# First layer of the NSA compression in a decoder trunk: one matmul of 512 columns for the high and low weights together, in place of two of 256

## The chip, the cores and the metric

The kernel runs on one core of one Trainium2 chip. The metric is device time in microseconds (us) for one execution: before the change the median of three runs is 1060.82 us (1060.35 to 1060.99). The profiled execution, from which all durations here are read, took 1061.77 us, with a span of 1060.0 us between its first and its last instruction.

The engines are named as in the profile: PE is the matmul engine (PEld its weight loads), DVE the vector engine, ACT the scalar engine, POOL and SP the two that mostly start transfers. The profile's "x" behind a row counts instructions, and a pair such as 128x512 gives partitions and elements of each.

## The reference, cut to what matters

One layer of a decoder trunk for 256 positions and 2048 channels in fp32: a normalised input goes through one wide projection `w_in`; three branches (a linear recurrence, A; sparse attention in the NSA manner, B; attention with a forget gate, C) each give 1024 channels; each branch is multiplied by its own gate, projected by `w_branch`, weighted by a merge gate, and the sum goes through `w_out`. The change lies in branch B, in the compressed blocks:

```python
def compress(t, pos, w1, w2):
    ...
    blocks = jnp.concatenate([chunks[:, r:r + n_cmp] for r in range(ratio)], axis=2)
    blocks = blocks + pos[:, None, :]
    flat = blocks.transpose(0, 1, 3, 2, 4).reshape(b, n_cmp, hk, CMP_BLOCK * dk)
    return jax.nn.silu(flat @ w1) @ w2
...
    k_c = rms_norm(compress(split_heads(z['nsa_k_cmp'], NSA_KV_HEADS), cmp_pos[l, 0],
                            cmp_w1[l, 0], cmp_w2[l, 0]), nsa_k_gain[l])
    v_c = compress(split_heads(z['nsa_v_cmp'], NSA_KV_HEADS), cmp_pos[l, 1],
                   cmp_w1[l, 1], cmp_w2[l, 1])
```

There are 15 blocks for each of 2 heads; `w1` is 4096 x 256, once for keys and once for values. Branch A's output, which matters for what follows, is `rglru_branch(...) * silu(z['lru_gate'])`, and it is the first that is projected.

## The kernel before, in words

**Numbers in two parts.** A fp32 product is made of the short format's matmuls: each operand is split into a high part (ACT rounds a copy) and a low part (DVE subtracts it from the original), and high·high, high·low and low·high are summed in PSUM (`mm3`, line 384).

**Pieces.** All weights come as one stream of pieces of at most 128x1024 (`plan`, line 76). A piece is loaded into `raw`, split into `wh` (ACT) and `wl` (DVE) by `cut` (line 418), and used by a few matmuls. Splitting runs three pieces ahead of use (`AHEAD`), in four buffers each for `wh` and `wl`. ACT's part is issued at the start of a piece; DVE's subtraction of the same later piece is put off to the middle of the current piece (`low_parts`, line 413). A piece of 512 columns by 2 rows of blocks has 12 matmuls.

**The first layer of the compression** (lines 1350 to 1361) is spread between the pieces of `w_in`: 8 pieces for keys, then 8 for values, each with 4 blocks of 128 rows by 256 columns. Its input `k_xs` has 60 columns, 30 high and 30 low ones, so that one matmul against `wh` and one against `wl` give all products; both accumulate in one half of a PSUM bank, keys in columns 0 to 255, values in 256 to 511. When the values are done, `cmp_end` (line 829) copies the bank to `hs`, transposes it, adds the 30 low rows to the 30 high ones, and goes on to the second layer.

**Side work and its order.** Everything that isn't a weight piece (recurrence, norms, attention, splitting of the branch outputs) is written as tasks that are advanced in small steps. Instructions stand in each engine's queue in the order in which this program writes them, so the order is fixed when the kernel is built. A clock in the kernel (`Clock`, line 158) adds up a cost for each instruction on each engine. After the first half and at the end of every piece, `Side.tick` (line 257) gives each urgent and each active task one step, unless that clock holds DVE or ACT to be further behind PE than a limit (`LIMITS`: 3000 ns for urgent tasks, 2500 ns for the others, from the first attention queries on). Tasks also wait by that clock until what they need would be done.

**What a piece needs.** Before a piece is written, `need` (line 1281) looks whether the tasks whose results it reads have been written, and if not, it steps all tasks regardless of the limit until they are:

```python
        for name in wait:
            n = 0
            while name not in side.done:
                n += 1
                assert n < 2000, name
                clock.t["pe"] += 200.0
                side.tick(True)
```

**The first projection.** `ysplit0` (`y_split`, line 1102) makes branch A's output: in four quarters of 128x512, DVE multiplies `k_yl` by the gate `k_gl`, ACT rounds it to `k_yh`, and DVE subtracts to `k_yl` (another buffer of that name). A quarter may be written once the four `lru` tasks are done. The first column block of `w_branch` has four pieces, and piece number i needs quarter number i. Ahead of that block stands the first block of merge gates, whose result DVE and ACT turn into `k_mg` (line 1213).

Of the kernel before, what the change touches and what calls it, by code (L numbers as in the profile page):

```python
# [11 lines left out]
R32 = mybir.dt.float32r  # L12
AF = mybir.ActivationFunctionType
OP = mybir.AluOpType
AX = mybir.AxisListType

P = 128
# [9 lines left out]
NCMP = 15  # L27
NR = 32
HID = 256
# [296 lines left out]
def block_kernel(ctx: ExitStack, tc: tile.TileContext, io):  # L326
    nc = tc.nc
    clock = Clock()
    V, A, T, G, Q = (Metered(e, clock, n) for e, n in ((nc.vector, "v"), (nc.scalar, "a"), (nc.tensor, "pe"),
                                                      (nc.gpsimd, "g"), (nc.sync, "d")))  # L330
    pool = lambda name, bufs=1, **k: ctx.enter_context(tc.tile_pool(name=name, bufs=bufs, **k))
    cp = pool("cp")
    wp = pool("wp")
# [11 lines left out]
    def nm(s):  # L345
        uid[0] += 1
        return f"{s}_{uid[0]}"
# [7 lines left out]
    def two(shape, dt=F32, name="b2"):  # L355
        return k2.tile(shape, dt, tag="k2", name=nm("k2_" + name))
# [7 lines left out]
    def f(ap):  # L364
        return ap.bitcast(F32)

    mains = [pp.tile([P, 512], F32, name=f"main{i}") for i in range(4)]
    banks = [pp.tile([P, 512], F32, name=f"bank{i}") for i in range(4)]
# [12 lines left out]
    def split(hi, lo, src, scale=None):  # L381
        splits((hi, lo, src, scale))
# [11 lines left out]
    def parts_of(h, k, nk):  # L394

        n = h["n"]
        if h is halves[0] and k == 0:
            return [(0, n // 2), (n // 2, n)]
        return [(k * n, (k + nk) * n)]
# [13 lines left out]
    def low_parts():  # L413

        while due:
            V.tensor_tensor(*due.pop(0), op=OP.subtract)

    def cut(h, k=0, nk=None, late=False):
        m, n = h["nk"] * h["n"], h["n"]
        nk = nk or h["nk"]  # L420
        if k == 0:
            h["whl"] = [wp.tile([P, 1024], R32, tag=x, bufs=AHEAD + 1, name=nm(x)) for x in ("wh", "wl")]
        wh, wl = h["whl"]
        for a, b in parts_of(h, k, nk):
            if late:
                A.activation(wh[:, a:b], h["raw"][:, a:b], AF.Copy)
                due.append((wl[:, a:b], h["raw"][:, a:b], f(wh[:, a:b])))
            else:
                split(wh[:, a:b], wl[:, a:b], h["raw"][:, a:b])
        h["wh"] = wh[:, :m].rearrange("p (k n) -> p k n", n=h["n"])  # L430
        h["wl"] = wl[:, :m].rearrange("p (k n) -> p k n", n=h["n"])
# [44 lines left out]
    def halves_of(pairs_):  # L476
        return lambda k: (pairs_[k // 8][0][:, k % 8, :], pairs_[k // 8][1][:, k % 8, :])


    st = {}  # L480
# [29 lines left out]
    for i in range(4):  # L510
        for k in range(2):
            if i < FINE or k == 0:
                n = 1 if i < FINE else 2
# [315 lines left out]
    def cmp_end():  # L829
        b = st["cmpb"]  # L830
        w2 = two([P, 2, 2, P], name="w2")
        G.dma_start(w2, io["w2"])
        hs = two([4 * NCMP, 512], name="hs")
        A.activation(hs, banks[b][:4 * NCMP, :], AF.Copy)
        yield from side.settle()

        for q in range(4):
# [3 lines left out]
        hz = banks[b][:, :4 * 4 * NCMP].rearrange("p (q s i) -> p q s i", q=4, s=2)  # L841
# [14 lines left out]
        for q in range(2):  # L856
            T.matmul(banks[b][:64, 256:256 + P], hid2[:, q].rearrange("p g c i -> p (g c i)"), w2[:, 1, q, :],
                     start=q == 0, stop=q == 1)
# [438 lines left out]
    def prepare(j):  # L1297

        for ks in ([0], [1]) if j < FINE else (range(2),):
            if "pair" in halves[j]:  # L1300
                hn_first(halves[j]["pair"], ks)
            if j < FINE:
                cut(halves[j], ks[0], 1)
        if j >= FINE:
            cut(halves[j], late="q0" in side.done)
# [4 lines left out]
    for i, h in enumerate(halves):  # L1310
# [28 lines left out]
        if kind == "ple":  # L1339
            out = by_rows(h, lambda k: (pTh[:, k, :], pTl[:, k, :]))  # L1340
        elif kind in ("rows", "turned"):
            out = by_rows(h, halves_of(hn))
        elif kind == "proj":
            out = by_rows(h, lambda k: (st["ys"][0][:, k, :], st["ys"][1][:, k, :]))
        elif kind == "out":
            out = by_rows(h, halves_of(st["mt"]))
        elif kind == "gate":
            out = by_rows(h, halves_of(st["ht"]))
        else:
            kv = h["key"]  # L1350
            if h["first"] and kv == 0:
                st["cmpb"] = side.free.pop(0)[0]
            for k in range(h["nk"]):
                if 2 * k == h["nk"]:
                    low_parts()
                for q, w in enumerate((h["wh"], h["wl"])):
                    T.matmul(banks[st["cmpb"]][:4 * NCMP, kv * HID:(kv + 1) * HID], st["xs"][kv][:, h["k"] + k, :],
                             w[:, k, :], start=h["first"] and k == 0 and q == 0 and kv == 0,
                             stop=h["last"] and k == h["nk"] - 1 and q == 1 and kv == 1)
            if h["last"] and kv == 1:  # L1360
                side.urge("cmpend", cmp_end())
        if h["last"]:
# [28 lines left out]
RAW, LOADS, AHEAD = 6, 7, 3  # L1391
# [88 lines left out]
```

## Time and profile before

| | before |
|---|---|
| median of three runs | 1060.82 us |
| the profiled execution | 1061.77 us |
| its span | 1060.0 us |
| PE busy | 1053.3 us (99%) |
| DVE busy | 772.2 us (73%) |
| ACT busy | 620.6 us (59%) |
| granted clock | 0.999 |

Matmuls overlap in their pipeline: a row of 512 columns lasts 0.39 us, but the next one starts 0.227 us later. So PE's share of busy time says little, and the distance from one start to the next is what has to be read. The chain of waits (the work that ended last, followed backwards) names runs of matmuls by where they write: "main" for the four banks of the weight pieces, "bank" for the four that side work and the first layer of the compression use. A line of the program is of no use as a key, since one helper records every instruction (L208); groups are told apart by the names of the tiles.

### The profile page before, as it was taken

To read this page: it belongs to the slowest core of one execution; us is meant where nothing else is said; L and a number is where in the kernel's file an instruction comes from. 1 tells how busy PE (TensorE), PEld (TensorE's weight loads), DVE (VectorE), ACT (ScalarE), POOL (GpSimd) and SP (SyncE) were. 2 spreads that over 40 slices of the span, in tenths; PEclk is the share of its full clock that TensorE was granted. 3 is DMA by queue.
4 is the path that set the end of the run, shared out by engine and by line. 5 is a ranking of instruction groups with operands and counts; after the bars stand their busy time and mean duration, and the time that the engine had idled before them with its cause. 6 is when DMAs were issued, how large, how long until landed. Compare 5 with 4: busy or idle time off the path is not lost.

```text
span 1060.0 us, 14061 instructions
## 1 busy us (share of the span) xinstructions
PE 1053.3 (99%) x4903; PEld 879.3 (83%) x4903; DVE 772.2 (73%) x1151; ACT 620.6 (59%) x940; POOL 53.1 (5%) x77
## 2 busy tenths in 40 slices
PE   9999999999999999999999999999999999999998
PEld 7888889888888888888888888888888888888886
DVE  7777889897778678678987965555766566766664
ACT  7668877768766667544645644555555444444442
POOL 0000001110000000020110000000001000000000
PEclk9999999999999999999999999999999999999999
DMA  9767868787657467577677566766676877778751
GB/s 337 248 201 260 257 200 280 233 266 226 217 189 218 150 198 216 182 234 251 194 235 239 186 222 207 223 213 214 219 244 196 264 235 220 236 250 257 278 207 60
DMA packets 86295, 237.52 MB, mean 224 GB/s; under 512 B 14024, under 2 KB 31312, under 8 KB 86224
## 3 DMA queue, kind: packets, MB, share of 16 engines
q1 hardware_dynamic: 81504, 220.87, 64.8%
q0 software_dynamic: 4720, 15.76, 5.5%
q8 instruction: 38, 0.62, 0.3%
q14 instruction: 33, 0.27, 0.1%
HBM read 215.61 MB, written 4.20 MB: 207 GB/s over the span
## 4 chain that ended last, share of the span: by engine, by line
PE 91%; DVE 3%; DMA 2%; ACT 2%; SPq 1%; issue 1%; DVEq 0%; ACTq 0%
PE main L208 87%; PE bank L208 4%; SPq L208 1%; DVE wl L208 1%; DMA raw<-in_w 1%; DMA k_fpz<-k_fprob 1%; DMA k_pz<-k_prob 1%; ACT wh L208 0%; ACT k_pz L208 0%; DVE k_fq L208 0%; DVE k_prob L208 0%; DVE k_fprob L208 0%; DVE k_pt L208 0%; DVE k_fbias L208 0%; DVE k_fx L208 0%
## 5 line engine op out<-in xcount | busy, mean ns | idle before, releaser
L208 DVE TENSOR_TENSOR wl<-raw,wh 128x1024 fp32r<-128x1024 f32 (+2 forms) x388 | 459.8, 1197 | 186.0 <-ACT wh L208 185.2
L208 ACT ACTIVATE wh<-raw 128x1024 fp32r<-128x1024 f32 (+2 forms) x388 | 400.2, 1040 | 318.3 <-PE main L208 281.3
L208 PE MATMUL main<-wh,k_hnh 128*128 128x512 f32 (+2 forms) x1026 | 395.0, 385 | 0.5 <-ACT wh L208 0.5
L208 PE MATMUL main<-wh,k_hnl 128*128 128x512 f32 (+1 forms) x1024 | 393.0, 384 | 0.0
L208 PE MATMUL main<-wl,k_hnh 128*128 128x512 f32 (+2 forms) x1026 | 392.9, 384 | 0.0
L208 PEld LDWEIGHTS main<-wh,k_hnh 128*128 128x128 f32 x1026 | 193.2, 189 | 37.5 <-ACT wh L208 1.1
L208 PEld LDWEIGHTS main<-wh,k_hnl 128*128 128x128 f32 x1024 | 192.5, 188 | 38.1
L208 PEld LDWEIGHTS main<-wl,k_hnh 128*128 128x128 f32 x1026 | 193.2, 189 | 35.9 <-DVE wl L208 0.2
L208 PE MATMUL main<-wl,k_yh 128*128 128x512 f32 x192 | 74.9, 390 | 0.1
L208 PE MATMUL main<-wh,k_yh 128*128 128x512 f32 x192 | 74.9, 390 | 0.0
L208 PE MATMUL main<-wh,k_yl 128*128 128x512 f32 x192 | 74.8, 389 | 0.0
L208 PE MATMUL main<-wh,k_mth 128*128 128x512 f32 x128 | 49.8, 389 | 0.0
L208 PE MATMUL main<-wl,k_mth 128*128 128x512 f32 x128 | 49.8, 389 | 0.0
L208 PE MATMUL main<-wh,k_mtl 128*128 128x512 f32 x128 | 49.8, 389 | 0.0
L208 PE MATMUL main<-wh,k_hth 128*128 128x512 f32 x128 | 49.8, 389 | 0.0
L208 PE MATMUL main<-wl,k_hth 128*128 128x512 f32 x128 | 49.8, 389 | 0.0
L208 PE MATMUL main<-wh,k_htl 128*128 128x512 f32 x128 | 49.8, 389 | 0.0
L208 PEld LDWEIGHTS main<-wl,k_yh 128*128 128x128 f32 x192 | 36.0, 188 | 7.7 <-DVE wl L208 0.5
L208 PEld LDWEIGHTS main<-wh,k_yl 128*128 128x128 f32 x192 | 36.0, 188 | 7.5
L208 PEld LDWEIGHTS main<-wh,k_yh 128*128 128x128 f32 x192 | 36.1, 188 | 7.4
L208 ACT ACTIVATE k_mg<-k_mg 128x512 f32<-128x512 f32 x24 | 15.2, 633 | 26.6 <-DVE k_mg L208 26.3
L208 PEld LDWEIGHTS main<-wl,k_mth 128*128 128x128 f32 x128 | 24.0, 188 | 5.0
(243 smaller groups left out, 948.4 us busy)
## 6 DMA issues: line engine op xcount, KB each, us to landing
raw<-in_w SPq DMA_DIRECT2D x369, 512.0 KB, 4.5
bias<-in_b_in POOLq DMA_DIRECT2D x21, 256.0 KB, 5.2
raw<-in_w SPq DMA_DIRECT2D x8, 408.0 KB, 4.0
k_pz<-k_prob SPq DMA_DIRECT2D x16, 128.0 KB, 4.2
e_dram<-k_e POOLq DMA_DIRECT2D x4, 512.0 KB, 3.6
k_merged<-k_zt SPq DMA_DIRECT2D x16, 128.0 KB, 3.2
k_xc<-in_x POOLq DMA_DIRECT2D x4, 512.0 KB, 6.4
k_hx<-k_zt SPq DMA_DIRECT2D x16, 128.0 KB, 3.6
```

The source lines that it names most:

```text
L208: r = call(out, *args, **kw)
```

## The change

`wh` and `wl` become the two halves of one tile `whl`. The first layer's two matmuls for a block of 128 rows become one with 512 moving columns, the 256 high and the 256 low weights, and its 512 results fill the whole bank: high products in the left half, low ones in the right. So keys and values can't share the bank any more. After the last piece of the keys, and again after that of the values, ACT copies the left half to `hs` and DVE adds the right half; `hs` is now taken before the first piece, and its copy in `cmp_end` is gone.

```diff
@@ cut
-            h["whl"] = [wp.tile([P, 1024], R32, tag=x, bufs=AHEAD + 1, name=nm(x)) for x in ("wh", "wl")]
-        wh, wl = h["whl"]
+            h["whl"] = wp.tile([P, 2, 1024], R32, tag="whl", bufs=AHEAD + 1, name=nm("whl"))
+        wh, wl = h["whl"][:, 0], h["whl"][:, 1]
@@ cmp_end
-        hs = two([4 * NCMP, 512], name="hs")
-        A.activation(hs, banks[b][:4 * NCMP, :], AF.Copy)
+        hs = st["hs"]
@@ the pieces of the first layer
                 st["cmpb"] = side.free.pop(0)[0]
+                st["hs"] = two([4 * NCMP, 512], name="hs")
+            hz = banks[st["cmpb"]][:4 * NCMP, :].rearrange("p (s n) -> p s n", s=2)
             for k in range(h["nk"]):
                 if 2 * k == h["nk"]:
                     low_parts()
-                for q, w in enumerate((h["wh"], h["wl"])):
-                    T.matmul(banks[st["cmpb"]][:4 * NCMP, kv * HID:(kv + 1) * HID], st["xs"][kv][:, h["k"] + k, :],
-                             w[:, k, :], start=h["first"] and k == 0 and q == 0 and kv == 0,
-                             stop=h["last"] and k == h["nk"] - 1 and q == 1 and kv == 1)
+                T.matmul(hz, st["xs"][kv][:, h["k"] + k, :], h["whl"][:, :, k * HID:(k + 1) * HID],
+                         start=h["first"] and k == 0, stop=h["last"] and k == h["nk"] - 1)
+            if h["last"]:
+                part = st["hs"][:, kv * HID:(kv + 1) * HID]
+                A.activation(part, hz[:, 0], AF.Copy)
+                V.tensor_tensor(part, part, hz[:, 1], op=OP.add)
```

Because the kernel's own clock counts the shorter first layer and the two additions, the steps of the side work fall at other places from the first layer on, until some 640 us into the span. Three places show what the prediction speaks of.

First, PE's queue at the first piece of the first layer, before the change. `k_xs` is the input in its 60 columns, and the rows read "output <- weights, input":

```order
L208 MATMUL main_84<-wh_721,k_hnl_129 128x512
L208 MATMUL bank_90<-wh_743,k_xs_644 60x256
L208 MATMUL bank_90<-wl_744,k_xs_644 60x256
L208 MATMUL bank_90<-wh_743,k_xs_644 60x256
L208 MATMUL bank_90<-wl_744,k_xs_644 60x256
L208 MATMUL bank_90<-wh_743,k_xs_644 60x256
L208 MATMUL bank_90<-wl_744,k_xs_644 60x256
L208 MATMUL bank_90<-wh_743,k_xs_644 60x256
L208 MATMUL bank_90<-wl_744,k_xs_644 60x256
L208 MATMUL main_83<-wh_765,k_hnh_128 128x512
```

And the same place after it:

```order
L208 MATMUL main_84<-whl_696,k_hnh_128 128x512 x2
L208 MATMUL main_84<-whl_696,k_hnl_129 128x512
L208 MATMUL bank_90<-whl_717,k_xs_622 60x512 x4
L208 MATMUL main_83<-whl_738,k_hnh_128 128x512 x2
L208 MATMUL main_83<-whl_738,k_hnl_129 128x512
```

Eight matmuls of 256 columns have become four of 512; nothing else moved here.

Second, DVE's queue around the first projection, before the change. `k_yl<-k_yl,k_gl` is the multiplication of a quarter, `k_yl<-k_yl,k_yh` its low part, `wl<-raw,wh` the low part of a weight piece, `k_mg` the merge gates. The first pair is that of the fourth quarter; the other three stand further up:

```order
L208 TENSOR_TENSOR k_yl_567<-k_yl_567,k_gl_980 128x512
L208 TENSOR_TENSOR k_yl_2769<-k_yl_567,k_yh_2768 128x512
L208 TENSOR_TENSOR wl_2912<-raw_2818,wh_2911 128x1024
L208 SCALAR_TENSOR_TENSOR k_mg_2930<-main_85,rsr,bias_2796 128x512
L208 SCALAR_TENSOR_TENSOR k_mg_2931<-main_86,rsr,bias_2796 128x512
L208 TENSOR_TENSOR wl_2939<-raw_2839,wh_2938 128x1024
L208 TENSOR_TENSOR wl_2957<-raw_2857,wh_2956 128x1024
L208 TENSOR_TENSOR wl_2975<-raw_2883,wh_2974 128x1024
```

After it. The first two quarters stand ahead of these rows, and the pairs shown are those of the third and the fourth; `sp_sm`, `k_pc` and `k_pz` belong to a step of an attention task:

```order
L208 SCALAR_TENSOR_TENSOR k_mg_2787<-main_86,rsr,bias_2650 128x512
L208 TENSOR_TENSOR whl_2794<-raw_2702,whl_2794 128x1024
L208 TENSOR_TENSOR whl_2811<-raw_2727,whl_2811 128x1024
L208 TENSOR_TENSOR k_yl_548<-k_yl_548,k_gl_936 128x512
L208 TENSOR_TENSOR k_yl_2755<-k_yl_548,k_yh_2754 128x512
L208 TENSOR_SCALAR sp_sm_2564<-sp_sm_2564 128x6
L208 RECIPROCAL sp_sm_2564<-sp_sm_2564 128x6
L208 TENSOR_TENSOR sp_sm_2564<-sp_sm_2564,bg 128x6
L208 SCALAR_TENSOR_TENSOR k_pc_361_2566<-sp_pc_2565,sp_sm_2564,k_pc_361_2566 128x2x16
L208 TENSOR_SCALAR k_pz_2568<-k_pz_2568,sp_sm_2564 128x4x32 x2
```

The last two rows come once more, and then the two of the fourth quarter. Two of the four quarters have moved from ahead of the merge gates to behind them and behind two low parts of weight pieces, and a step of attention stands between the two.

Third, PE's queue where the third piece of the first projection begins, after the change (`kk` are keys, `k_qh` and `k_ql` queries):

```order
L208 MATMUL main_84<-whl_2746,k_yl_2755 128x512
L208 MATMUL bank_87<-kk,k_qh_2490 128x272 x2
L208 MATMUL bank_87<-kk,k_ql_2491 128x272
L208 MATMUL bank_89<-kk,k_qh_2490 128x256 x2
L208 MATMUL bank_89<-kk,k_ql_2491 128x256
L208 MATMUL main_83<-whl_2768,k_yh_2754 128x512 x2
L208 MATMUL main_83<-whl_2768,k_yl_2755 128x512
```

Before the change that piece follows the second one directly:

```order
L208 MATMUL main_84<-wh_2885,k_yh_2768 128x512
L208 MATMUL main_84<-wl_2886,k_yh_2768 128x512
L208 MATMUL main_84<-wh_2885,k_yl_2769 128x512
L208 MATMUL main_83<-wh_2911,k_yh_2768 128x512
L208 MATMUL main_83<-wl_2912,k_yh_2768 128x512
L208 MATMUL main_83<-wh_2911,k_yl_2769 128x512
```

Six matmuls of an attention task now stand between the second and the third piece; they and the third quarter's three steps come from one turn that `need` has forced, the only one in the program (before the change there is none).

## The prediction

> **What bounds the kernel now.** I read the page first, then the chain of waits in order of time, then the first layer's tile, then the timeline of each engine around the first projection. From the page, the engines and the chain:
>
> ```profile
> PE 1053.3 (99%) x4903; PEld 879.3 (83%) x4903; DVE 772.2 (73%) x1151; ACT 620.6 (59%) x940; POOL 53.1 (5%) x77
> PE 91%; DVE 3%; DMA 2%; ACT 2%; SPq 1%; issue 1%; DVEq 0%; ACTq 0%
> ...
> L208 PE MATMUL main<-wh,k_hnh 128*128 128x512 f32 (+2 forms) x1026 | 395.0, 385 | 0.5 <-ACT wh L208 0.5
> ```
>
> PE is 91% of the chain, and its largest group of matmuls was kept waiting for 0.5 us in all (the figure behind the second bar). Whether it ever stands still otherwise shows in its starts. Stretches of the chain in order of time (start, duration, what, how many), with a piece of the compression's first layer in "bank" and ordinary weight pieces in "main":
>
> ```profile
> 84.48 0.95 PE bank L208 x8
> ...
> 187.77 0.93 PE bank L208 x8
> 188.71 8.19 PE main L208 x36
> 196.89 0.93 PE bank L208 x8
> ```
>
> 36 matmuls of 512 columns take 8.19 us, 0.2275 each; eight of 256 take 0.93, 0.1163 each; and 187.77 + 0.93 + 8.19 is the start of the next, so nothing stands between. PE is the bound, and a microsecond of matmuls saved or of waiting added there is a microsecond of the run, as long as nothing else is touched.
>
> **The shorter first layer.** How often such a stretch occurs, from the input tile's groups (shortest, median, longest duration in ns):
>
> ```profile
> L208 PE MATMUL bank<-wh,k_xs x64: 276/278/283, 79.3 to 225.1; 128*60 128x256 f32 x64
> L208 PE MATMUL bank<-wl,k_xs x64: 274/279/283, 79.4 to 225.2; 128*60 128x256 f32 x64
> ```
>
> 128 matmuls are 16 stretches of eight. After the change each is four of 512 columns: 4 x 0.2275 = 0.91 us in place of 0.93. By these rounded rows that saves 16 x 0.02 = 0.3 us; the one at 84.48 reads 0.95, which would make it 16 x 0.04 = 0.6. I take 0.4 us. The 512 columns lie in two runs of 256, 1024 apart; no row isolates what that costs, and I take nothing.
>
> [...]
>
> **The additions.** ACT's copy of 60x512 goes, and for keys and for values come a copy of 60x256 and a DVE addition of 60x256. The row that goes, and the nearest rows for what comes:
>
> ```profile
> L208 ACT ACTIVATE k_hs<-bank x1: 571/571/571, 226.5 to 226.5; 60x512 f32<-60x512 f32 x1
> L208 ACT ACTIVATE k_lru<-bank,vec 64x256 f32<-64x256 f32 x32 | 15.0, 467 | 0.7 <-PE bank L208 0.2
> L208 DVE TENSOR_TENSOR k_fq<-k_fq,bank 128x256 f32<-128x256 f32 x8 | 3.3, 413 | 0.6 <-ACT k_fq L208 0.6
> L208 PEld LDWEIGHTS bank<-idr,k_hs x4: 135/138/139, 231.3 to 231.5; 60*128 60x128 f32 x4
> ```
>
> ACT gains 2 x 0.47 - 0.57 = 0.4 us of work and DVE 2 x 0.41 = 0.8. The first values' matmul overwrites the bank, so it now waits for the keys' addition; a stretch of the first layer comes only every 9 us or so (187.77, 196.89), so 0.9 us of work is long done. At the end, the transposes started at 231.3, 4.8 us after the copy, so the longer 0.9 us has cover too. I take nothing for either; without that cover each would cost its 0.9 us.
>
> **What the moved side work does.** This is the term that decides. Before the change all four quarters of branch A's output are written ahead of the merge gates. After it the third and fourth come behind them. DVE's timeline before, then ACT's, then PE's:
>
> ```profile
> 293.39 0.69 DVE L208 TENSOR_TENSOR k_yl<-k_yl,k_gl 128x512 f32<-128x512 f32 x1
> 294.77 0.69 DVE L208 TENSOR_TENSOR k_yl<-k_yl,k_yh 128x512 fp32r<-128x512 f32 x1 [0.70 <-ACT k_yh L208]
> 295.38 1.22 DVE L208 TENSOR_TENSOR wl<-raw,wh 128x1024 fp32r<-128x1024 f32 x1
> 296.52 1.40 DVE L208 SCALAR_TENSOR_TENSOR k_mg<-main,rsr,bias 128x512 f32<-128x512 f32 x2
> 299.57 1.23 DVE L208 TENSOR_TENSOR wl<-raw,wh 128x1024 fp32r<-128x1024 f32 x1 [1.65 <-ACT wh L208]
> 300.71 1.22 DVE L208 TENSOR_TENSOR wl<-raw,wh 128x1024 fp32r<-128x1024 f32 x1
> ```
>
> ```profile
> 294.11 0.63 ACT L208 ACTIVATE k_yh<-k_yl 128x512 fp32r<-128x512 f32 x1 [1.10 <-DVE k_yl L208]
> 297.30 1.29 ACT L208 ACTIVATE k_mg<-k_mg 128x512 f32<-128x512 f32 x2 [2.55 <-DVE k_mg L208]
> 298.50 2.94 ACT L208 ACTIVATE wh<-raw 128x1024 fp32r<-128x1024 f32 x3
> ```
>
> ```profile
> 294.42 0.39 PE L208 MATMUL main<-wh,k_yh 128*128 128x512 f32 x1
> 299.86 0.39 PE L208 MATMUL main<-wh,k_yh 128*128 128x512 f32 x1
> 303.94 0.41 PE L208 MATMUL bank<-kk,k_qh 128*128 128x272 f32 x2
> 304.69 0.41 PE L208 MATMUL bank<-kk,k_qh 128*128 128x272 f32 x2
> ```
>
> The first projection starts at 294.42; a piece of 12 matmuls takes 2.72 us, so its third starts at 294.42 + 5.44 = 299.86, as the second row shows. DVE is late there: the merge gates had to wait for the banks and for the quarter ahead of them, ACT's rounding of the next weights waited behind the gates, and DVE's two low parts behind ACT's. The second of them ends at 300.71 + 1.22 = 301.93, 2.07 us after PE has reached the third piece.
>
> After the change the third quarter stands exactly there, behind the second low part. I put the changed queues on this clock. The multiplication starts at 301.85 (DVE's rows overlap by 0.1). From the first rows, ACT begins 0.72 us after the multiplication, DVE's low part 1.38 after it, and the quarter's high part is ready at +1.35 (294.11 + 0.63 - 293.39), its low part at +2.07. ACT is free at 301.44. So the high part is there at 303.2, the low at 303.9. PE has only the six attention matmuls ahead, 0.75 us (304.69 - 303.94), and would begin at 300.6: it waits 2.6 us. Its third matmul reads the low part, 0.45 us later, at 303.65, and waits another 0.25. That is 2.85 us.
>
> The fourth quarter comes behind a step of attention. DVE's rows for that step, first and last:
>
> ```profile
> 313.73 0.17 DVE L208 TENSOR_SCALAR sp_sm<-sp_sm 128x6 f32<-128x6 f32 x1
> 315.50 0.48 DVE L208 TENSOR_SCALAR k_pz<-k_pz,sp_sm 128x128 f32<-128x128 f32 x2
> ```
>
> The step takes 315.98 - 313.73 = 2.25 us, so the fourth multiplication starts at 303.9 + 2.2 = 306.1 and its high part is ready at 307.45. PE, from 303.2 on, needs 2.72 + 0.25 for the third piece and stands at 306.15: it waits 1.3, and 0.25 again for the low part, 1.55 us.
>
> Sum: 2.85 + 1.55 - 0.4 = +4.0 us. Nothing behind gives it back, since PE has no pause to fill. I add 0.1 us for semaphores between the engines: **+4.1 us**. Queued behind the waiting matmuls on PE is all the rest of the program; DVE and ACT meanwhile catch up, so no third wait follows: the next low part, `whl_2828`, is wanted a whole piece later.
>
> Bounds of this term. If DVE had no work left when PE reaches the third piece, the high part would be there 1.35 us later and the first wait 0.6 in place of 2.6; the rest stays: +2.1. If DVE were 1.6 us further behind (as it is one piece earlier: 299.57 + 1.23 ends 3.66 us after 297.14), +5.7. The quarter ahead of the merge gates is written at the same place in both programs, so DVE's state there should be what these rows show, and I take it unchanged.
>
> The rest of the side work, from 80 to 640 us, changes places too. The steps that decide here, the quarters and the step of attention, issue no transfers, so SP's and POOL's queues keep what they have around them. Elsewhere PE has only the half microsecond of the first fence to win; I take nothing, with 0.5 us either way.
>
> The profiled execution took 1061.77 us, so its like would take 1065.9; the median is 0.95 lower, and the forecast for it is 1060.82 + 4.1 = **1064.9 us**.
>
> **The rivals.**
> *The quarters come in time.* If the third multiplication began by 299.2, 0.6 us before the third piece, and the fourth likewise, PE would wait for neither, and only the saved 0.4 us is left: 1060.4 us, not slower. It decides at 2.6 us less on DVE than the rows show. Against it, the low parts wait for ACT behind the merge gates, which wait for PE's own matmuls: DVE can't get far ahead there.
> *DVE has no queue, but the quarters still pass through DVE, ACT and DVE.* The lower bound above: 1062.9 us. For it: DVE is idle for 1.65 us shortly before. Against it: what ended that pause was ACT, with two more low parts to follow.
> *PE's clock falls during the wait.* At the start PE runs slowly after standing idle:
>
> ```profile
> 4.07 0.80 PE L208 MATMUL main<-wh,k_hnh 128*128 128x256 f32 x2
> 8.11 0.63 PE L208 MATMUL main<-wl,k_hnh 128*128 128x512 f32 x1
> 8.54 0.63 PE L208 MATMUL main<-wh,k_hnl 128*128 128x512 f32 x1
> 9.33 0.39 PE L208 MATMUL main<-wl,k_hnh 128*128 128x512 f32 x1
> ```
>
> Starts of 512 columns are 0.43 us apart there, not 0.2275, from 4.07 to about 9.3. If the wait threw PE back into that for 5.2 us, it would do 5.2 x 0.2275 / 0.43 = 2.75 us of work in it and lose 2.4: 1067.3 us. Against it: the wait is 2.6 us long, not as long as the idle time before the kernel. [...]
> *Another place in the moved side work* adds or takes a microsecond or more; by the bounds of the wait above, 1.6 to 2 us each, two such places give 1058 to 1068 us.
>
> **How the numbers follow.** The forecast, with its bounds short of the no-queue case, has 0.67; in time 0.06; no queue 0.13; the clock 0.08; another place 0.06. A measurement of this kernel can tell 0.2%, 2.1 us, from no change: slower begins at 1062.9. The forecast and the clock lie above it, half of the no-queue case (0.06) and half of another place (0.03) as well: slower 0.84. Faster ends at 1058.7, which only another place could reach: 0.02. The same: 0.14. The range leaves out the case in time, the clock and some of another place, under 0.2, and takes in the bounds: 1062.5 to 1067.0.
>
> **What would show it.** In the changed profile, the stretches of the first layer read x4 and 0.91 us. In the timeline near 300 us, PE's first matmul of the third piece carries a wait on ACT's `k_yh` of about 2.6 us, and that of the fourth one of about 1.3; DVE's `k_yl` stands behind two `whl` rows. If PE's starts there are 0.23 apart, I am wrong about DVE's state; if the waits are there but the time isn't longer, some pause elsewhere has gone; if 0.43 us separates the starts behind the wait, the clock fell.

## The result, and the profile after

| | before | after |
|---|---|---|
| median | 1060.99 us (5 runs, 1060.35 to 1062.33) | 1067.79 us (5 runs, 1067.15 to 1068.33) |
| ratio | | 1.0061 [1.0047, 1.0075] |
| the profiled execution, its span | 1061.77 us, 1060.0 us | 1067.15 us, 1065.3 us |

Slower by 6.8 us, where 4.1 was forecast; 1067.79 lies above the range, which ended at 1067.0. The page of the changed kernel, in the rows that answer to those of before (busy us, then behind the second bar the idle time ahead of the group):

```profile
PE 1054.0 (99%) x4839; PEld 873.8 (82%) x4839; DVE 773.9 (73%) x1153; ACT 619.9 (58%) x941; POOL 50.1 (5%) x77
PE 94%; DVE 3%; DMA 1%; SPq 1%; issue 1%; ACT 0%; DVEq 0%; ACTq 0%
L208 PE MATMUL main<-whl,k_yh 128*128 128x512 f32 x384 | 120.2, 394 | 4.4 <-ACT k_yh L208 4.4
```

The shares tell nothing new; the last row has a wait of 4.4 us on `k_yh`, the high part of a quarter, which the kernel before did not have. PE's timeline there, the first matmuls of the first projection, then from the last attention matmuls ahead of its third piece on:

```profile
295.36 0.62 PE L208 MATMUL main<-whl,k_yh 128*128 128x512 f32 x2
...
301.39 0.41 PE L208 MATMUL bank<-kk,k_qh 128*128 128x272 f32 x2
...
306.70 1.22 PE L208 MATMUL main<-whl,k_yh 128*128 128x512 f32 x2 [4.43 <-ACT k_yh L208]
307.73 0.63 PE L208 MATMUL main<-whl,k_yl 128*128 128x512 f32 x1
308.15 1.05 PE L208 MATMUL main<-whl,k_yh 128*128 128x512 f32 x2
309.00 0.63 PE L208 MATMUL main<-whl,k_yl 128*128 128x512 f32 x1
...
311.15 0.62 PE L208 MATMUL main<-whl,k_yh 128*128 128x512 f32 x2
```

The wait stands where it was forecast, on what was forecast, and is 4.43 us long, not 2.6. Behind it three starts take 1.27 us (307.73 to 309.00), 0.42 each, and from about 310.2 on 0.23. The piece lasts from 306.70 to 311.15, 4.45 us in place of 2.72, and the fourth begins without a wait. The granted clock in three stretches of 3.4 us (length, PE busy, granted clock):

```profile
303.30:306.74 3.44, 0.04 (x1) 1.00 0.60 174
306.74:310.15 3.41, 3.41 (x8) 0.50 0.57 201
310.15:313.56 3.41, 3.41 (x16) 1.00 0.00 0
```

So the clock was halved for one stretch of 3.41 us, from the end of the wait on: 1.7 us of work lost in it. Wait and slow piece are 6.2 us; the spans of the profiled pair differ by only 5.3. Where the rest lies shows in PE's starts. For each matmul I take the distance from its start to the next one, less the median distance for its shape over the kernels, and add these up by stretches of the span (us):

| stretch | before | after |
|---|---|---|
| 0 to 20 | 5.4 | 5.0 |
| 20 to 290 | 2.0 | 1.8 |
| 290 to 320 | 0.0 | 7.1 |
| 320 to 500 | 1.9 | 0.6 |
| behind 500 | 0.9 | 1.0 |

The changed order thus loses 7.1 us around the first projection and wins 1.3 us behind it, where the kernel before has small delays ahead of attention matmuls (0.3 us near 406, for one). At the start the clock came up earlier in this execution, at 6.37 us and not 9.24, and PE reached the first layer at 78.91, against 79.29 before.

DVE's timeline tells why the quarters came late, the rows on the quarters and the splits ahead of them:

```profile
279.32 1.27 DVE L208 TENSOR_TENSOR_SCAN k_yl<-k_lru,k_lru 128x256 f32<-128x256 f32 x2
...
285.64 1.22 DVE L208 TENSOR_TENSOR whl<-raw,whl 128x1024 fp32r<-128x1024 f32 x1 [2.29 <-ACT whl L208]
...
293.72 0.69 DVE L208 TENSOR_TENSOR k_yl<-k_yl,k_gl 128x512 f32<-128x512 f32 x1
...
296.85 0.68 DVE L208 TENSOR_TENSOR k_yl<-k_yl,k_gl 128x512 f32<-128x512 f32 x1
...
298.85 1.22 DVE L208 TENSOR_TENSOR whl<-raw,whl 128x1024 fp32r<-128x1024 f32 x1
299.98 1.40 DVE L208 SCALAR_TENSOR_TENSOR k_mg<-main,rsr,bias 128x512 f32<-128x512 f32 x2
303.03 2.36 DVE L208 TENSOR_TENSOR whl<-raw,whl 128x1024 fp32r<-128x1024 f32 x2 [1.64 <-ACT whl L208]
305.30 0.69 DVE L208 TENSOR_TENSOR k_yl<-k_yl,k_gl 128x512 f32<-128x512 f32 x1
```

And the kernel before, DVE's last scan of the recurrence and its first and third quarter:

```profile
262.95 1.27 DVE L208 TENSOR_TENSOR_SCAN k_yl<-k_lru,k_lru 128x256 f32<-128x256 f32 x2
...
276.64 0.68 DVE L208 TENSOR_TENSOR k_yl<-k_yl,k_gl 128x512 f32<-128x512 f32 x1
...
283.25 0.68 DVE L208 TENSOR_TENSOR k_yl<-k_yl,k_gl 128x512 f32<-128x512 f32 x1
```

The recurrence's last scan, which every quarter needs, stands 16 us later (279.32 for 262.95), and the first quarter 17 us (293.72 for 276.64). Most of the scan's delay is one pause of its task: between two of its steps on ACT, `k_lru<-k_lru,spn` and `k_uc<-k_lru`, lie 11.0 us (259.33 to 270.35), and 1.1 before (255.39 to 256.51). Why the kernel's clock gave it no step in that time is not traced. Between scan and first quarter DVE waits 2.29 us for ACT, whose queue has the softmax of an attention task there, with a table load; the weight split that DVE waits for ends at 284.56 + 1.04 = 285.60:

```profile
280.19 1.28 ACT L208 ACT_TABLE_LOAD   x1
281.80 0.51 ACT L208 ACTIVATE k_pz<-k_prob,sp_m 128x128 f32<-128x128 f32 x1
284.56 1.04 ACT L208 ACTIVATE whl<-raw 128x1024 fp32r<-128x1024 f32 x1
```

The changed order thus put attention where the quarters had stood. DVE's second low part ends at 305.39, 4.00 us after PE reached the third piece (301.39). The prediction took 2.07.

The rows account for the 1.93 us in between. Right ahead of the gates now stand two quarters, each with a low part of a weight piece behind it, where the kernel before has one: 3.13 us more (293.72 to 296.85). DVE came to the first of the two 1.64 us ahead of the projection's start, and before to the one there 1.03 us ahead (293.39 and 294.42), which gives back 0.61. And PE, which got the low parts of the first two quarters only just in time (the second ends at 298.93 and is first read at 298.99), took 6.03 us for the first two pieces (295.36 to 301.39) in place of 5.44, so the gap closes by another 0.59.

The first layer itself, from the chain of waits:

```profile
98.27 0.92 PE bank L208 x4
...
107.37 0.92 PE bank L208 x4
```

x4, as said, but 0.92, not 0.91. From first start to the first behind it, the 16 stretches sum to 14.93 us before and 14.83 after by rows rounded to 0.01; by the trace's own times, kept to the nanosecond, to 14.95 and 14.80. So 0.15 us was won, not 0.4. The stretch of the chain at 84.48, which the prediction counted as one of the first layer, is none: before the change there stand, at that place of PE's timeline, eight matmuls of the recurrence, and after it they take the same 0.95 us (84.09).

```profile
84.32 1.11 PE L208 MATMUL bank<-k_ucs,k_wds 128*128 128x256 f32 x8
```

### The profile page after: what moved, and what is told of

Same layout as the page of the kernel before. It is cut to its first block, busy times and chain, and to the rows that moved or that the text cites. A ratio compares the mean times of both kernels' runs of the same rounds, so it can differ in the third digit from the quotient of the medians.

```text
span 1065.3 us, 13940 instructions
## 1 busy us (share of the span) xinstructions
PE 1054.0 (99%) x4839; PEld 873.8 (82%) x4839; DVE 773.9 (73%) x1153; ACT 619.9 (58%) x941; POOL 50.1 (5%) x77
## 4 chain that ended last, share of the span: by engine, by line
PE 94%; DVE 3%; DMA 1%; SPq 1%; issue 1%; ACT 0%; DVEq 0%; ACTq 0%
PE main L208 90%; PE bank L208 4%; DVE whl L208 1%; SPq L208 1%; DMA k_fpz<-k_fprob 1%; DMA raw<-in_w 0%; DVE k_fq L208 0%; DVE k_fprob L208 0%; DVE k_fpz L208 0%; DVE k_fbias L208 0%; DVE k_fx L208 0%; ACT whl L208 0%; DVE k_fin L208 0%; DVE k_fk L208 0%; DVE sp_nss L208 0%
## 5 line engine op out<-in xcount | busy, mean ns | idle before, releaser
L208 PE MATMUL main<-whl,k_hnh 128*128 128x512 f32 (+2 forms) x2052 | 619.1, 384 | 0.7 <-ACT whl L208 0.5
L208 DVE TENSOR_TENSOR whl<-raw,whl 128x1024 fp32r<-128x1024 f32 (+2 forms) x388 | 460.1, 1198 | 186.6 <-ACT whl L208 182.6
L208 ACT ACTIVATE whl<-raw 128x1024 fp32r<-128x1024 f32 (+2 forms) x388 | 401.1, 1041 | 322.1 <-PE main L208 281.7
L208 PEld LDWEIGHTS main<-whl,k_hnh 128*128 128x128 f32 x2052 | 379.2, 188 | 76.5 <-ACT whl L208 1.4
L208 PE MATMUL main<-whl,k_hnl 128*128 128x512 f32 (+1 forms) x1024 | 392.3, 383 | 0.0
L208 PEld LDWEIGHTS main<-whl,k_hnl 128*128 128x128 f32 x1024 | 192.3, 188 | 37.8
L208 PE MATMUL main<-whl,k_yh 128*128 128x512 f32 x384 | 120.2, 394 | 4.4 <-ACT k_yh L208 4.4
L208 PE MATMUL main<-whl,k_mth 128*128 128x512 f32 x256 | 78.8, 389 | 0.0
L208 PE MATMUL main<-whl,k_hth 128*128 128x512 f32 x256 | 78.8, 389 | 0.0
L208 PE MATMUL main<-whl,k_yl 128*128 128x512 f32 x192 | 75.5, 393 | 0.0
```

The lines of the kernel that those rows point to most:

```text
L208: r = call(out, *args, **kw)
```

## The experiments

Theory after the comparison: the loss is all in the order of the side work; the change of the first layer is worth nothing either way. Rival: the matmul of 512 columns, the shared tile or the additions cost something.

**The order or the matmul.** old_order keeps the change, but the kernel's own clock is charged as before, so that all else stands in the order of before:

```diff
                 T.matmul(hz, ...)
+                clock.t["pe"] += 13.4
...
-                A.activation(part, hz[:, 0], AF.Copy)
-                V.tensor_tensor(part, part, hz[:, 1], op=OP.add)
+                nc.scalar.activation(part, hz[:, 0], AF.Copy)
+                nc.vector.tensor_tensor(part, part, hz[:, 1], op=OP.add)
```

> The change's own matmuls, tile and additions are kept (the first layer in one matmul of 512 columns, high and low weights in one tile, the halves added on ScalarE and VectorE), but the program's clock is charged as the kernel before charged it, so that everything else stands in the order of the kernel before. Theory: the whole loss is in the order; the stretches of the first layer are 0.4 us shorter together, no wait of over 1 us ends on k_yh in the first projection, and the time is about 1060.5 us (1060.0 to 1061.2). Rival: the matmul of 512 columns or the one tile for both halves has a cost of its own (a buffer that comes free later, the additions on the path): then over 1062 us although the order is the old one.

Measured: 1060.85 us (11 runs), ratio 0.9994 [0.9986, 1.0003], no wait over 0.8 us; its 16 stretches are 0.1 us shorter than before, not 0.4. two_again keeps the new order and goes back to two matmuls of 256 columns:

```diff
-                T.matmul(hz, x, w, ...)
+                for q in range(2):
+                    nc.tensor.matmul(hz[:, q], x, w[:, q], ...)
+                clock.add("pe", 512 / 2.4 + 13.4, hz, [x, w])
```

> The opposite half: the order of the changed kernel to the instruction, with the first layer in two matmuls of 256 columns again. Theory: the wait of 4.4 us on k_yh at the third piece of the first projection stays and the first layer's 0.4 us come back, so about 1068.2 us (1067.2 to 1069.0). Rival (the 512-column matmul itself costs): back towards 1061 us.

Measured: 1067.74 us (5 runs), ratio 1.0063 [1.0049, 1.0076], and the same wait of 4.44 us. The order alone makes the loss; the rival has fallen. The first layer's gain is too small for these times to show.

**The clock.** keep_warm fills the wait with matmuls:

```diff
+            if h["key"] == 0 and h["nth"] == 2:
+                for _ in range(19):
+                    nc.tensor.matmul(mains[2], hn[0][0][:, 0, :P], h["wh"][:, 0, :], start=True, stop=True)
```

> The changed kernel with 19 matmuls of 512 columns, into a bank that is overwritten afterwards, between the second and the third piece of the first projection; they ask for nothing that is late and take 19 x 0.2275 = 4.3 us, about as long as the wait on k_yh. All other engines keep their order. Theory: PE is busy through the wait, so the granted clock stays at 1.0 and the third piece's matmuls start 0.2275 us apart (0.43 us in the changed kernel for 3.4 us); the fourth quarter's wait, which the slow clock hid, then shows with 1.0 to 1.5 us, so the time falls by only 0.2 to 0.8 us, to 1067.0 to 1067.6. Rival (the slow clock has nothing to do with PE's wait): the same 3.4 us at 0.43 us between starts in the trace, and no wait at the fourth piece.

Measured: 1066.69 us (1066.53 to 1066.87), ratio 1.0051 [1.0038, 1.0064]. PE's timeline:

```profile
302.02 4.49 PE L1345 MATMUL main<-whl,k_hnh 128*128 128x512 f32 x19
306.62 0.73 PE L208 MATMUL main<-whl,k_yh 128*128 128x512 f32 x2
307.35 0.50 PE L208 MATMUL main<-whl,k_yl 128*128 128x512 f32 x1
310.71 0.73 PE L208 MATMUL main<-whl,k_yh 128*128 128x512 f32 x2 [0.79 <-ACT k_yh L208]
```

No half clock (the run's mean granted clock is 0.999, the changed kernel's 0.998), and the fourth quarter's wait appears, with 0.79 us. So PE's idleness brought the slow clock, and the slow clock hid the fourth wait. Net of that it cost about 1.1 us by the medians (the ratios differ by 0.0010), where 0.2 to 0.8 was expected. In the two profiled executions it cost nothing: from the projection's first start to the first one behind its fourth piece are 18.53 us here (295.31 to 313.84) and 18.54 in the changed kernel (295.36 to 313.90). The 1.1 us would then lie in executions of the changed kernel that weren't profiled, three of which have a lower mean clock (0.995 to 0.997, against 0.998); that is not shown.

**Why DVE is late.** exps_out takes ACT's exponentials out of the attention steps just ahead of the projection. It leaves out that part of the computation: POOL sets the results and their sums to 1.0.

```diff
-                A.activation(o, x, AF.Exp, bias=m[:, a, i:i + 1], scale=-1.0, accum_out=s[:, a, i:i + 1])
+                if 109 <= st["piece"] <= 112:
+                    clock.add("a", ...)
+                    nc.gpsimd.memset(o, 1.0)
+                    nc.gpsimd.memset(s[:, a, i:i + 1], 1.0)
+                else:
+                    A.activation(o, x, AF.Exp, ...)
```

> The changed kernel without ScalarE's exponentials (and their sums) of the attention steps that are written during the pieces 109 to 112, just ahead of the first projection; GpSimd sets the tiles to 1.0 in their place, and PE's and VectorE's orders stay to the instruction. That part of the computation is left out. Theory: ScalarE, which was at work without a pause from 279 to 293 us, made VectorE late for the weight splits and so for the quarters; with 9 exponentials and their table load less (about 4 us of ScalarE) VectorE stands about 1.9 us earlier, the wait on k_yh is 2.4 to 3.0 us instead of 4.4, the clock does not fall, the fourth quarter's wait shows with about 1.3 us, and the time is about 1.5 to 3 us under the changed kernel's, 1064.8 to 1066.3. Rival (VectorE is late for a cause that lies elsewhere, its own queue or the weights' transfers): the wait stays at 4.0 to 4.6 us and the time at 1067 to 1068.

Measured: 1064.37 us, ratio 1.0028 [1.0017, 1.0039]. The wait shrank by 1.85 us, as the theory said: DVE's second low part ends at 302.73, 2.15 us after PE reached the third piece (300.58). The table load, which was expected to go as well, only came later, at 282.87. That the clock would not fall was wrong, and the time lies a little under what was expected:

```profile
304.04 0.73 PE L208 MATMUL main<-whl,k_yh 128*128 128x512 f32 x2 [2.58 <-ACT k_yh L208]
...
305.22 1.06 PE L208 MATMUL main<-whl,k_yh 128*128 128x512 f32 x2
306.07 0.63 PE L208 MATMUL main<-whl,k_yl 128*128 128x512 f32 x1
```

Behind this wait of 2.58 us the granted clock was 0.50 for one stretch (304.96 to 308.38). warm_exps adds keep_warm's matmuls, 11 of them, so that both premises of the prediction hold (the exponentials are missing here too).

> The prediction's own sum with both of its premises put in place: exps_out (the same part of the computation missing), so that VectorE is about 2 us behind at the third piece and not 4, and 11 matmuls as in keep_warm (11 x 0.2275 = 2.5 us) through the wait of 2.6 us, so that the clock stays up. Theory (the sum of the prediction was right but for these two): starts 0.2275 us apart behind the third piece, a wait on k_yh of 0.8 to 1.4 us at the fourth, which the half clock hid in exps_out, and a time within 0.6 us of exps_out's 1064.4, 1063.6 to 1064.8, over the kernel before by 2.4 to 3.6 us. Rival (the fourth quarter is on time, and the wait there in keep_warm came from the later VectorE): no wait at the fourth piece, 1062.3 to 1063.3.

Measured: 1064.03 us, ratio 1.0026 [1.0016, 1.0036], 1.7 to 3.8 us over before, with 0.85 us at the fourth piece. With its premises in place the forecast of +4.1 is too high, but not at its own place. From the projection's first start to the first one behind its fourth piece, less the attention matmuls that lie in it, are 15.44 us, and 10.90 before: 4.5 more, which is what the prediction's terms for that place make (2.85, 1.55 and 0.1). What the time is lower by was won elsewhere, in its profile above all between 320 and 500 us, where PE's starts lose 0.7 us, and 1.9 before.

**Why the quarters are late.** quarters_first steps `ysplit0` at every turn:

```diff
     def tick(self, hurry=False):
...
+        for task in [t for t in self.urgent if t[0] == "ysplit0"]:
+            try:
+                next(task[1])
...
```

> The changed kernel, with the steps of the four quarters of branch A taken at every turn whatever the clock says, so that the third and fourth quarter stand ahead of the merge gates on VectorE again. Theory: PE has no wait over 1 us at the third and fourth piece of the first projection, the clock does not fall there, and the time is about 1060.6 us (1060.0 to 1061.6). Rival (other side work that has also moved costs as well, or something else pays for the quarters coming first): the wait goes but the time stays at 1063 us or more.

Measured: 1064.36 us (1062.84 to 1065.59), ratio 1.0024 [1.0013, 1.0035]. The rival holds: the wait on `k_yh` is gone, but a weight split is late in its place:

```profile
297.98 0.50 PE L208 MATMUL main<-whl,k_yh 128*128 128x512 f32 x1 [2.10 <-DVE whl L208]
```

quarters_exps joins quarters_first and exps_out (with the exponentials missing).

> Both causes taken away at once: the four quarters ahead of the gates, as in quarters_first, and ScalarE's 18 exponentials and sums of pieces 109 to 112 left out, as in exps_out (that part of the computation is missing). Theory: each alone leaves a wait of its own in the first projection (2.1 us on a weight split, 2.6 us on k_yh); together nothing is late, PE has no wait over 0.5 us from 290 to 320 us, the clock stays at 1.0 there, and the time is 1060.3 to 1061.3 us, that of the kernel before within 0.6. Rival (a third cause: VectorE's own additional work in that stretch, or other moved steps, cost as well): a wait of 1 us or more is left and the time is 1062 us or more.

Measured: 1062.36 us, ratio 1.0013 [1.0004, 1.0022]; again the rival. 1.97 us of wait on a split are left, and DVE's timeline shows what stands ahead of it:

```profile
291.55 0.68 DVE L208 TENSOR_TENSOR k_yl<-k_yl,k_gl 128x512 f32<-128x512 f32 x1
292.93 0.69 DVE L208 TENSOR_TENSOR k_yl<-k_yl,k_yh 128x512 fp32r<-128x512 f32 x1 [0.70 <-ACT k_yh L208]
...
294.92 0.69 DVE L208 TENSOR_TENSOR k_yl<-k_yl,k_yh 128x512 fp32r<-128x512 f32 x1 [0.70 <-ACT k_yh L208]
295.53 3.49 DVE L208 TENSOR_TENSOR whl<-raw,whl 128x1024 fp32r<-128x1024 f32 x3
```

Two quarters in a row hold DVE for 4 us, 1.4 of it waiting for ACT's rounding. The recurrence's scan stands at 278.58 here, so its lateness may be why they bunch. lru_first, which leaves nothing out, takes the last two recurrence tasks at every turn as well (the edit is against quarters_first):

```diff
-        for task in [t for t in self.urgent if t[0] == "ysplit0"]:
+        first = ("ysplit0", "lru3", "lru2")
+        for group in (self.active, self.urgent):
+            for task in [t for t in group if t[0] in first]:
```

> quarters_first, with the last two recurrence tasks of branch A (whose scans the quarters need, at 279 us in the changed kernel, at 264 before) also taken at every turn whatever the clock says. Nothing is left out. The four quarters then stand among the weight splits of the end of w_in, and a step of attention stands where they were. Theory (the last cause is that the recurrence came late, so that the quarters bunched on VectorE ahead of the splits of the first projection): the fourth quarter is done by about 290 us, no wait over 0.6 us at the first projection, no half clock, and 1060.3 to 1061.3 us, the kernel before's time within 0.6. Rival (the attention steps that now stand ahead of the merge gates make the splits late all the same): a wait of 1 us or more there and 1062 us or more.

Measured: 1074.24 us, ratio 1.0118 [1.01, 1.0137]. The first projection has no wait at all, but nearly all of PE's waits on DVE's splits came elsewhere, between 126 and 173 us, where the steps were now forced on DVE (us in total, times, longest):

```profile
PE main L208 <- DVE whl L208: 8.9, 7, 2.9
```

So the time answered another question than was asked. lru_late puts the recurrence ahead only once the first attention queries are done (the edit is against lru_first):

```diff
-        first = ("ysplit0", "lru3", "lru2")
+        first = ("ysplit0", "lru3", "lru2") if "q0" in self.done else ("ysplit0",)
```

> As lru_first, but the last recurrence task is put ahead only from the first attention queries on (from about 250 us), so that nothing is forced between 110 and 250 us. Nothing is left out. Theory (the late recurrence, with the quarters behind it, is the whole of the loss at the first projection): the last scan stands near 262 us as in the kernel before, the quarters before 285 us, no wait over 0.6 us from 250 to 320 us, no half clock there, and 1060.3 to 1061.5 us. Rival (whatever is put ahead on VectorE makes a split late, as in lru_first): a wait of 1 us or more between 250 and 320 us and 1062 us or more.

Measured: 1061.27 us (11 runs), ratio 1.0001 [0.9992, 1.001]. The scan stands at 247.75, earlier than expected, the last quarter is done at 263.8, there is no wait at the first projection and no half clock (mean granted clock 1.0). The longest wait on a split is 0.63 us, at 247.9. With the recurrence and the quarters in time the loss at the first projection is gone, although the rest of the side work stands in neither kernel's order: from its first start to the first one behind its fourth piece, less attention, are 10.97 us; the kernel before takes 10.90 and the changed one 17.80. That the whole time comes out equal as well is in part chance. PE's starts lose 2.0 us more than before between 230 and 290 us, where those steps were now put ahead, and 1.2 less between 320 and 500.

**The price of a wait.** Into the kernel before, ahead of another projection's third piece, a wait of a chosen length (7 memsets here, in wait_mid; 2 in wait_tiny, 4 in wait_short, 13 in wait_long):

```diff
+                nc.tensor.matmul(banks[0], hold[:, :P], hold, start=True, stop=True)
+                for _ in range(7):
+                    nc.gpsimd.memset(f(hold), 0.0)
+                nc.tensor.matmul(banks[0], hold[:, :P], hold, start=True, stop=True)
```

> The kernel before with a wait put into PE's queue ahead of a projection far from the change (the tenth projection's third piece): PE reads a tile, 4 memsets on GpSimd of 128x512 (about 0.56 us each) overwrite it, PE reads it again. Nothing is left out. [...] Rival (any wait of PE over 2 us brings the slow clock): 0.43 us between starts for some us behind it, +4.3 us, 1065.3.

> As wait_short, with 7 memsets: a wait of about 4.2 us. [...]

> [...] Theory: the clock falls every time, a stretch of at least 1 us and at most 3.4 us behind the wait at 0.43 us between starts, +7.6 us and 0.5 to 1.7 us on top, 1069.0 to 1070.2. Rival: no slow clock behind it, 1068.5.

> As wait_short, with 2 memsets: a wait of about 1.3 us. What the longer ones showed: apart from the wait the insertion itself took 1.6 us of PE (two matmuls, a wait of 0.4 us for the first), and the clock halved for the rest of the next stretch of 3.41 us of a fixed grid when PE had been busy in a stretch for 37% or less, not at 52%. Theory (that threshold): a wait of 1.3 us and one of 0.4 leave every stretch busy for at least 50%, so no half clock in any run, starts of 0.2275 us behind it, and +2.9 us against the kernel before, about 1064.5, with runs close together. Rival (any wait of over 1 us can halve the clock): half clock in the trace, +4.5 us, 1066.

| | wait | median | over before | less the wait and 1.4 us of insertion |
|---|---|---|---|---|
| wait_tiny | 1.2 us | 1064.54 us | 3.3 us | 0.7 us |
| wait_short | 2.4 us | 1067.56 us | 5.9 us | 2.1 us |
| wait_mid | 4.1 us | 1068.92 us | 7.3 us | 1.8 us |
| wait_long | 7.6 us | 1072.84 us | 11.2 us | 2.2 us |

PE's timeline in wait_tiny, from the last matmul ahead of the insertion to the first behind it:

```profile
784.72 0.39 PE L208 MATMUL main<-wh,k_hnl 128*128 128x512 f32 x1
785.47 0.50 PE L1345 MATMUL bank<-k_hold 128*128 128x512 f32 x1 [0.36 <-DVE k_hold L1344]
787.20 0.50 PE L1348 MATMUL bank<-k_hold 128*128 128x512 f32 x1 [1.22 <-POOL k_hold L1347]
787.54 0.40 PE L208 MATMUL main<-wh,k_hnh 128*128 128x512 f32 x1
```

The two starts lie 2.82 us apart in place of 0.23: 1.22 of wait and 1.4 for the insertion itself. What is left is the slow clock: 1.8 to 2.2 us behind the waits of 2.4, 4.1 and 7.6 us. The profiles of the three have it. wait_short's shows two stretches at a granted clock of 0.50 behind its wait of 2.39 us, so the theory of 1063.6 us without a slow clock fell, and its rival holds there (the profile is of the longest of its runs, 1070.59 us). The times of all three lie above what was expected with the slow clock (1065.3 us for wait_short, 1067.0 for wait_mid, 1069.0 to 1070.2 for wait_long), which counted nothing for the insertion and, in wait_short's rival, one slow stretch where the profile shows two. wait_tiny's profile has no slow stretch (mean granted clock 0.999), but three of its six runs lie at 1064.9 to 1066.0 us with a mean granted clock of 0.997, the others at 1063.9 to 1064.2 with 0.999 or more: "no half clock in any run" was probably wrong. The runs of quarters_first part in the same way. A second profile of each was to catch the longer case:

> quarters_first once more, for a second profile: its runs lay in two groups, 1062.8 to 1063.3 us with a mean granted clock of 0.999 to 1.0 and 1064.4 to 1065.6 with 0.997 to 0.998, and its profile was of the first. Theory (the wait of 2.1 us halves the clock or not, according to where it falls in the fixed grid of 3.41 us): a run of the second group shows one or two stretches of 3.41 us at a granted clock of 0.5 right at the end of that wait, a run of the first group none. Rival (the groups have another cause): a run of 1064.4 us or more without a half clock, and with another wait in the trace.

> wait_tiny once more for a second profile. Theory: if this run is of the group at 1064.9 to 1066.0 us (mean granted clock 0.997), a stretch of 3.41 us at a granted clock of 0.5 lies right behind the wait of 1.2 us; if it is of the group at 1063.9 to 1064.2, none. Rival: a long run without a half clock.

Both were of the shorter kind (1063.07 and 1064.26 us), without a half clock. That the longer runs are the half clock rests on their mean clock; none of them was profiled.

## Why the prediction was wrong

- **The first layer, -0.4 us:** right that it matters little, mis-sized: -0.15. It was read as differences of 0.02 and 0.04 from rows rounded to 0.01, and the row behind the 0.04 was not the first layer at all. The stretch at 84.48 holds eight matmuls of the recurrence.
- **The additions, nothing:** right; old_order has them and loses nothing.
- **Where the loss is:** right. The third quarter behind the gates and two low parts, PE waiting on `k_yh`. The chain was right as well: DVE 2.07 us behind gave a wait of 2.6; 4.00 behind, by the same step, gives 4.5, and 4.43 was measured. exps_out, with DVE 2.15 behind, gave 2.58, and warm_exps, with both premises, loses at that place the 4.5 us that the terms make. The 0.1 us among them for semaphores was an estimate that no run isolates.
- **The step that failed:** "The quarter ahead of the merge gates is written at the same place in both programs, so DVE's state there should be what these rows show, and I take it unchanged." One quarter stands ahead of the gates in both programs, but what stands ahead of that one had changed. The recurrence's scan had moved by 16 us, and with it the first and second quarter. The two now came behind an attention softmax that held ACT and so DVE's splits, and stood right at the gates. The queue was compared around the gates, and not 30 us further back. That put DVE 1.9 us further behind; the bound had allowed 1.6. lru_late, which takes this away, loses nothing at the projection.
- **The clock, a rival with 0.08:** it happened, at 1.7 us of work for one stretch (2.4 was reckoned). As it hid the fourth wait, less of it reached the time: 1.1 us by keep_warm's median, nothing in the profiled pair. The reason given against it, that the wait is only 2.6 us long, was wrong by itself: behind exps_out's 2.58 us the granted clock was 0.50 for one stretch; how long PE stood idle before the kernel no trace shows. The late DVE alone (keep_warm, 1066.69 us) and the slow clock with DVE as forecast (exps_out, 1064.37 us) both stay inside the range of 1062.5 to 1067.0; by these medians it took the two together to leave it.
- **The fourth wait, 1.3 us:** 0.79 in keep_warm and 0.85 in warm_exps; in the changed kernel the slow clock hid it.
- **Nothing elsewhere, with 0.5 us either way:** not right, and by luck to the forecast's good. The wait is the only one over 0.8 us, but the moved side work wins 1.3 us between 320 and 500. The five profiles with that part of the order as in the changed kernel lose 0.6 to 0.7 us there, the seven with the order of before 1.6 to 4.1.

So in the profiled pair the first projection takes 6.9 us more (17.80 for 10.90, less attention), where the terms made 4.5. Of the 2.4 us in between, DVE's state takes 1.9, and the first two pieces, whose quarters came just in time for the same reason, the rest. Some 1.6 us come back elsewhere, which makes the 5.3 of the spans. The medians differ by 6.8, with 5.0 to 8.0 by the interval, because the profiled execution before lies 0.8 us above its median and the one after 0.6 us below. What the longer executions lose more is open; a second slow stretch would fit their mean clock.

## What to carry to other kernels

Where a program writes its own order, follow a moved step back to what it needs, and that again, before taking an engine's state from the old trace: here the quarter's neighbours looked the same, and its source had moved by 16 us. A wait on PE is to be priced with the slow clock that may stand behind it: here the profiles have it behind waits of 2.39, 2.58, 4.14, 4.43 and 7.63 us (wait_short, exps_out, wait_mid, the changed kernel, wait_long), and not behind 2.10 in quarters_first or 1.22 in wait_tiny. It cost 1.8 to 2.2 us in the three kernels with the longer inserted waits, and less in the changed kernel (1.1 by keep_warm's median), where a wait that follows would have taken the time anyway. A saving of a fraction of a microsecond isn't worth a change that reshuffles the queues, unless the old order can be kept with it, as in old_order.

## What the runs showed of the clock

In the clock records of the two kernels' profiles the granted clock is 1.0 or 0.5, and changes only on a grid of 3.413 us: in the changed kernel it rose at 6.37 us, fell 300.373 us later, 88 stretches of 3.4133, and came back after one; in the kernel before it rose at 9.24 and fell 1047.892 us later, 307 stretches, behind PE's last matmuls. The rows that follow set the granted clock of a stretch beside PE's work in the one before. wait_short, in four stretches of the grid (length, PE busy, granted clock):

```profile
787.15:790.56 3.41, 1.28 (x5) 1.00 1.02 312
790.56:793.98 3.42, 2.81 (x7) 0.50 0.98 376
793.98:797.39 3.41, 3.41 (x10) 0.50 0.31 125
797.39:800.80 3.41, 3.41 (x17) 1.00 0.00 0
```

Behind a stretch that was busy for 37% the clock halved; it stayed halved behind one that was busy for 82%, and came back behind a full one. exps_out halves it behind 27%:

```profile
301.55:304.96 3.41, 0.92 (x3) 1.00 0.63 185
304.96:308.38 3.42, 3.42 (x9) 0.50 0.35 144
```

quarters_first, with a wait of 2.10 us across an edge of the grid, did not fall behind 52%:

```profile
294.10:297.51 3.41, 1.78 (x8) 1.00 0.36 141
297.51:300.92 3.41, 2.94 (x13) 1.00 0.45 150
```

Near that the busy time of the profile doesn't decide. lru_first lost its clock behind the same 1.78 us, and quarters_exps kept it behind 1.64, 48% (293.19 to 296.61):

```profile
167.60:171.01 3.41, 1.78 (x13) 1.00 0.50 161
171.01:174.43 3.42, 1.31 (x6) 0.50 0.24 38
```

So the profiles have two slow stretches behind a wait of 2.39 us (wait_short), one behind 4.43 (the changed kernel) and none behind 2.10 (quarters_first): the number doesn't follow the length alone. wait_long's profile has three (790.10 to 800.34, each at 0.50), half of them inside the wait of 7.63 us itself.
